# A gate table built from bfloat16 one-hots and a gate in three bfloat16 parts, one product moved from GpSimd to VectorE, and routing of one token block put first

## The chip, the core and the metric

The kernel runs on one NeuronCore of a Trainium2 chip. The metric is the device time of one execution in microseconds. TensorE is called PE below, VectorE DVE, ScalarE ACT, GpSimd POOL and SyncE SP, as in the profile. DVE, ACT, POOL and SP each take their instructions in the order in which the program put them.

## What is computed

One decoder block over 528 tokens (16 meta tokens and 512 of the sequence) of width 2048: a mixer (differential attention beside an mLSTM), then a PEER layer, both added to the residual stream, and a final RMS norm. The change lies in the PEER layer, which works on the 512 tokens that are kept:

```python
q = (ht @ w_q).reshape(T, PEER_HEADS, 2, PEER_SUB_DIM)            # 8 heads
s = jnp.einsum('thpd,hpnd->thpn', q, sub_keys)
s1, i1 = lax.top_k(s[:, :, 0], 16); s2, i2 = lax.top_k(s[:, :, 1], 16)
cand_s = s1[..., :, None] + s2[..., None, :]
cand_i = i1[..., :, None] * 128 + i2[..., None, :]
best_s, best_pos = lax.top_k(cand_s.reshape(T, 8, 256), 16)
idx = ...   # 128 experts of 16384 for a token
gate = jax.nn.softmax(best_s, axis=-1)
...
act = jax.nn.gelu(jnp.einsum('td,tkd->tk', hb, u[ib]), approximate=False)
y   = jnp.einsum('tk,tkd->td', gb * act, v[ib])
```

## The kernel before

Tokens lie in four blocks of 128. The kernel treats blocks 0 to 2 (384 tokens, `ND`) densely: it multiplies them with all 16384 rows of `u` and of `v`, and a table `G` holds each token's gate at the experts that it chose and zero elsewhere. Block 3 (128 tokens) is treated sparsely: for each of its 128 choices the rows of `u` are gathered by an indirect DMA on POOL's queue (`dgather`, 1 MB into one of three `ug` buffers), and DVE multiplies them with the token and sums up (`dmul`, a **dot**). Later the same is done with the rows of `v`.

The large matmuls are done in three passes of split float32 (`mm3`: high times high, high times low, low times high). So each weight tile of 1 MB comes in two halves, each loaded by SP into one of three `raw` buffers, rounded to a high part on ACT (`hid`, line 76) and subtracted on DVE to a low part (`lod`, line 77); five buffers hold high halves, and five low ones.

The stages that matter here:

- **Queries and routing.** `step(n)` for n = 2 to 15 multiplies a tile of `wq`; `scores` makes the scores of a head, and `bgstep` does one step of routing on DVE, ACT and POOL: the top 16 of two score rows, sums of candidates (`cd`, POOL), their top 16, and the expert numbers (`oh` on POOL, `ids` on DVE). There are 32 tasks, 8 heads by 4 blocks, in a pipeline of three. DVE's order in this stage is that of the code.
- **Chunks of `u`.** `u_chunk(c)` for c = 0 to 127 is 48 matmuls of 384 columns into one of two `pu` banks, a GELU on ACT (`at`, line 854) and a store into `Ad` in DRAM. The first chunks run beside what is left of routing, one `bgstep` each. Then come the exp and the sums of the gate, and transposes of expert numbers and gates (`n1T`, `n2T`, `ghT`, `glT`).
- **Gate table.** From then on each chunk is followed by about one gate group `gbuild(q)` of four tokens, 96 in all: `ebuild` compares an iota with the two halves of the expert number (`e`, `eq`, DVE), POOL multiplies `eq` with the high and the low part of the gate (`eg`), PE multiplies `e` with both (`pg`, four matmuls of 256 columns), ACT copies one half out and DVE adds the other (`stg`). After each eight groups SP stores `stg`, of which there is one buffer, into `Gd` (2 MB). The dots of block 3 are put between the chunks, about 1.2 a chunk. Here only PE and POOL keep the order of the code; a scheduler orders DVE, ACT and SP when the program is built.
- **Product with `v`.** `p_mul` multiplies `Ad` with `Gd` (`tm`, POOL), `p_split` splits the product (`ah` on ACT, `al` on DVE), and PE multiplies with all of `v` (`py`), while the gathered rows of `v` are added for block 3 on DVE (`y`).

Of the kernel before, what the change touches and what calls it, by code (L numbers as in the profile page):

```python
# [57 lines left out]
def body(tc, I, out):  # L58
    nc = tc.nc
    top = ExitStack()  # L60
    with top:
# [603 lines left out]
def rest(tc, I, out, L):  # L665
# [142 lines left out]
    n1T = up.tile([128, ND], F, name="n1T")
    n2T = up.tile([128, ND], F, name="n2T")
    ghT = up.tile([128, ND], R, name="ghT")  # L810
    glT = up.tile([128, ND], R, name="glT")
    bg = []
# [14 lines left out]

    nd = [0, 0]

    def dots(n):  # L830
        while nd[1] < min(n, 128):
            if nd[0] < 128 and nd[0] - nd[1] < 3:
                dgather(nd[0])
                nd[0] += 1
            else:
                dmul(nd[1])
                nd[1] += 1

    def step(n, mid=None):
        if n + 1 < len(sp):  # L840
# [16 lines left out]
    with tc.tile_pool(name="tk", bufs=1) as tk, \  # L857
# [33 lines left out]

        def head_tasks(h, b):
# [63 lines left out]
        pipe = [None, None]  # L956

        def bgstep():
            cur = bg.pop(0) if bg else None
            a, b = pipe  # L960
            if b:
                b[4]()
            topk16((cur[0]() if cur else []) + (a[2]() if a else []))
            if cur:
                cur[1]()
            if a:
                a[3]()
            pipe[:] = [cur, pipe[0]]
# [6 lines left out]
            for _ in range(1 + n % 2):  # L975
                bgstep()
        ci = 0
        while bg or pend or any(pipe):
            u_chunk(ci, mid)
            ci += 1  # L980
            bgstep()
        for g in (gsel, gs[:, 0], gs[:, 1], gs[:, 2]):
            g3 = g.rearrange("p (h k) -> p h k", h=PH)
            mx = tk.tile([128, PH], F, name="gmx", tag="gmx", bufs=2)
# [18 lines left out]
        for src, dst in ((n1s, n1T), (n2s, n2T), (gs, None)):  # L1003
            pt = ptr.tile([128, ND], F, name="ptt", tag="ptt")
            for b in range(3):
                nc.tensor.transpose(pt[:, 128 * b:128 * b + 128], src[:, b, :], ident)
            if dst is not None:
                nc.scalar.copy(dst, pt)
            else:
                nc.scalar.copy(ghT, pt)  # L1010
                nc.vector.tensor_tensor(glT, pt, ghT.bitcast(F), op=OP.subtract)

    with tc.tile_pool(name="gk", bufs=1, reuse_waits="tile") as gk, \
            tc.tile_pool(name="psg", bufs=2, space=PSUM) as psg, \
# [4 lines left out]

        def ebuild(q):  # L1020
            t0 = 4 * q
            e1 = gk.tile([128, 4, 128], R, name="e1", tag="e1", bufs=2)
            eq = gk.tile([128, 4, 128], F, name="eq", tag="eq", bufs=2)
            eg = gk.tile([128, 4, 2, 128], R, name="eg", tag="eg", bufs=2)
            io = bcast_mid(iota, 4)
            nc.vector.tensor_tensor(e1, io, bcast(n1T[:, t0:t0 + 4], 128), op=OP.is_equal)
            nc.vector.tensor_tensor(eq, io, bcast(n2T[:, t0:t0 + 4], 128), op=OP.is_equal)
            nc.gpsimd.tensor_tensor(eg[:, :, 0, :], eq, bcast(ghT[:, t0:t0 + 4].bitcast(F), 128), op=OP.mult)
            nc.gpsimd.tensor_tensor(eg[:, :, 1, :], eq, bcast(glT[:, t0:t0 + 4].bitcast(F), 128), op=OP.mult)
            ge[q] = e1, eg  # L1030

        def gbuild(q):
# [1 line left out]
            if r == 0:  # L1034
                stg[tg] = gk.tile([128, NK, TG], F, name="stg", tag="stg")
            e1, eg = ge.pop(q)
            pg = psg.tile([128, 4, 2, 128], F, name="pg", tag="pg")
            for j in range(4):
                nc.tensor.matmul(pg[:, j].rearrange("p a b -> p (a b)"), e1[:, j, :],  # L1039
                                 eg[:, j].rearrange("p a b -> p (a b)"), start=True, stop=True)  # L1040
            so = stg[tg][:, :, r:r + 4]
            nc.scalar.copy(so, pg[:, :, 0, :].rearrange("p j n -> p n j"))
            nc.vector.tensor_tensor(so, so, pg[:, :, 1, :].rearrange("p j n -> p n j"), op=OP.add)
            if r + 4 == TG:
                nc.sync.dma_start(Gd[tg, :, 0:NK, :], stg[tg])

# [15 lines left out]
    with ExitStack() as sV:  # L1062
# [279 lines left out]
```

## Time and profile before

| | |
|---|---|
| time, median of 3 runs (lowest to highest) | 3402.59 us (3402.31 to 3407.22) |
| the profiled execution: its own time, which is its span | 3404.6 us |
| PE busy | 3356.0 us, 99% |
| DVE busy | 2396.9 us, 70% |
| ACT busy | 1208.3 us, 35% |
| POOL busy | 1249.8 us, 37% |
| moved by DMA | 755.13 MB, mean 222 GB/s |

The busy share of an engine is a mean over stages with different limits, and the ends of matmuls are modelled in the trace, so the pace of PE is better read from the GELU that follows each chunk. The granted clock of PE is given as a share of its full 2.4 GHz; 0.5 is the lower of its two levels.

### The profile page before, as it was taken

How to read it: one execution, taken by the hardware profiler on the slowest of the kernel's cores; microseconds unless marked ns; L12 is line 12 of the kernel's file. 1: busy time of each engine (PE TensorE's matmuls, PEld its weight loads, DVE VectorE, ACT ScalarE, POOL GpSimd, SP SyncE). 2: the span in 40 equal slices, each digit the busy share in tenths (PEclk: the TensorE clock that was granted, in tenths of full speed). 3: DMA queues.
4: the chain of work that ended last, by engine and by line, in shares of the span. 5: the costliest groups of instructions: out<-in, count | busy, mean ns of one | idle time of the engine just before them, and what ended most of it. 6: DMA issues, size and time to landing. Idle time of an engine off the chain costs nothing.

```text
span 3404.6 us, 46653 instructions
## 1 busy us (share of the span) xinstructions
PE 3356.0 (99%) x17906; PEld 2983.9 (88%) x17910; DVE 2396.9 (70%) x3278; ACT 1208.3 (35%) x1851; POOL 1249.8 (37%) x1197
## 2 busy tenths in 40 slices
PE   8999999999998998999999999999999999999998
PEld 8888898888887798999999999998888888888887
DVE  7444444353467878888888888845788878888885
ACT  6443444352342224333333333332323333333333
POOL 2020111110025566655555555412444333334432
PEclk9999999999999999999999999999999999999999
DMA  4222221223442247888888888887878888888973
GB/s 151 75 69 75 67 76 63 69 69 118 169 147 80 80 133 252 305 313 320 299 332 304 311 300 319 317 274 256 312 290 315 307 316 306 306 310 307 330 291 140
DMA packets 225310, 755.13 MB, mean 222 GB/s; under 512 B 20640, under 2 KB 88736, under 8 KB 190272
## 3 DMA queue, kind: packets, MB, share of 16 engines
q1 hardware_dynamic: 106064, 402.82, 33.6%
q0 software_dynamic: 36864, 268.45, 20.3%
q10 hardware_dynamic: 82160, 80.90, 7.1%
q8 instruction: 140, 2.29, 0.3%
q14 instruction: 82, 0.67, 0.1%
HBM read 693.36 MB, written 58.72 MB: 221 GB/s over the span
## 4 chain that ended last, share of the span: by engine, by line
PE 88%; DVE 7%; POOL 3%; issue 1%; ACT 1%; DMA 1%; SPq 0%; DVEq 0%; ACTq 0%; POOLq 0%
PE py L1195 11%; PE py L1197 10%; PE py L1196 10%; PE pu L87 10%; PE pu L86 10%; PE pu L88 10%; PE ps L86 5%; PE ps L88 5%; PE ps L87 5%; PE po L742 2%; PE po L740 2%; PE po L741 2%; DVE ids L939 1%; PE pg L1039 1%; DVE lod L77 1%
## 5 line engine op out<-in xcount | busy, mean ns | idle before, releaser
L86 PE MATMUL pu<-hh,hid 128*128 128x384 f32 (+1 forms) x2272 | 786.0, 346 | 5.5 <-ACT at L854 5.5
L87 PE MATMUL pu<-hh,lod 128*128 128x384 f32 (+1 forms) x2272 | 788.2, 347 | 0.0
L88 PE MATMUL pu<-hl,hid 128*128 128x384 f32 (+1 forms) x2272 | 781.2, 344 | 0.0
L1195 PE MATMUL py<-hiv,ah 128*128 128x512 f32 x1536 | 613.0, 399 | 0.6 <-ACT at L854 0.6
L1197 PE MATMUL py<-hiv,al 128*128 128x512 f32 x1536 | 605.2, 394 | 0.0
L1196 PE MATMUL py<-lov,ah 128*128 128x512 f32 x1536 | 602.1, 392 | 0.0
L76 ACT CAST hiv<-rawv 128x1024 fp32r<-128x1024 f32 x256 | 268.6, 1049 | 522.1 <-PE py L1197 492.5
L76 ACT CAST hid<-rawd 128x1024 fp32r<-128x1024 f32 x284 | 297.0, 1048 | 426.2 <-DMA rawd<-in_u_dram 327.4
L77 DVE TENSOR_TENSOR lod<-rawd,hid 128x1024 fp32r<-128x1024 f32 x284 | 396.2, 1403 | 69.0 <-ACT hid L76 68.6
L86 PEld LDWEIGHTS pu<-hh,hid 128*128 128x128 f32 x2272 | 430.4, 189 | 15.7 <-ACT at L854 5.8
L88 PEld LDWEIGHTS pu<-hl,hid 128*128 128x128 f32 x2272 | 432.1, 190 | 10.2
L87 PEld LDWEIGHTS pu<-hh,lod 128*128 128x128 f32 x2272 | 430.6, 190 | 9.6
L86 PE MATMUL ps<-xh,hiz 128*128 128x256 f32 (+2 forms) x1280 | 410.6, 321 | 0.6 <-DVE qT L368 0.5
L1136 POOL DMA_INDIRECT vg<-in_vn_dram,ids x128 | 219.9, 1718 | 493.0 <-DVE y L1144 480.2
L88 PE MATMUL ps<-xl,hiz 128*128 128x256 f32 (+2 forms) x1280 | 392.6, 307 | 0.0
L87 PE MATMUL ps<-xh,loz 128*128 128x256 f32 (+2 forms) x1280 | 392.1, 306 | 0.0
L823 DVE SCALAR_TENSOR_TENSOR ug<-ug,h2n 128x2048 f32<-128x2048 f32 x128 | 314.1, 2454 | 92.2 <-DMA ug<-in_un_dram,idx 91.7
L1197 PEld LDWEIGHTS py<-hiv,al 128*128 128x128 f32 x1536 | 288.3, 188 | 75.2
L1196 PEld LDWEIGHTS py<-lov,ah 128*128 128x128 f32 x1536 | 288.3, 188 | 68.6
L1195 PEld LDWEIGHTS py<-hiv,ah 128*128 128x128 f32 x1536 | 288.3, 188 | 67.2 <-ACT at L854 0.9
L77 DVE TENSOR_TENSOR lov<-rawv,hiv 128x1024 fp32r<-128x1024 f32 x256 | 323.3, 1281 | 28.5 <-ACT hiv L76 28.3
L1144 DVE SCALAR_TENSOR_TENSOR y<-vg,wsel,y 128x2048 f32<-128x2048 f32 x127 | 336.1, 2646 | 0.0
(313 smaller groups left out, 4797.9 us busy)
## 6 DMA issues: line engine op xcount, KB each, us to landing
rawd<-in_u_dram SPq DMA_DIRECT2D x256, 512.0 KB
rawv<-in_v_dram SPq DMA_DIRECT2D x256, 512.0 KB
rawz<-in_wz_dram SPq DMA_DIRECT2D x98, 512.0 KB
Ad<-at ACTq DMA_DIRECT2D x128, 192.0 KB
Gd<-stg SPq DMA_DIRECT2D x12, 2048.0 KB
gt<-Gd ACTq DMA_DIRECT2D x32, 768.0 KB
av<-Ad ACTq DMA_DIRECT2D x64, 384.0 KB
rawwo<-in_wo_dram SPq DMA_DIRECT2D x40, 512.0 KB
```

Source lines behind the costliest of these rows:

```text
L76: nc.scalar.copy(hi, raw)
L77: eng.tensor_tensor(lo, raw, hi.bitcast(F), op=OP.subtract)
L86: nc.tensor.matmul(ps, a, xh[k][:, cs], start=(k == 0), stop=False)
L87: nc.tensor.matmul(ps, b, xh[k][:, cs], start=False, stop=False)
L88: nc.tensor.matmul(ps, a, xl[k][:, cs], start=False, stop=(k == KD - 1))
L740: nc.tensor.matmul(ps[tb], mh[n][:, sl], h, start=(n == 0), stop=False)
L823: nc.vector.scalar_tensor_tensor(ug, ug, 1.0, h2n, op0=OP.mult, op1=OP.mult, accum_out=act[:, k:k + 1])
L1136: nc.gpsimd.indirect_dma_start(out=vg, out_offset=None, in_=I["vn"], in_offset=bass.IndirectOffsetOnAxis(ap=ids2[:, k:k + 1], axis=0))
L1144: nc.vector.scalar_tensor_tensor(y[:, 3, :], vg, wsel[:, k:k + 1], y[:, 3, :], op0=OP.mult, op1=OP.add)
L1195: nc.tensor.matmul(ps[tb], ah[:, sl], h, start=(pr + j == 0), stop=False)
L1196: nc.tensor.matmul(ps[tb], ah[:, sl], l, start=False, stop=False)
L1197: nc.tensor.matmul(ps[tb], al[:, sl], h, start=False, stop=(2 * pr + j == GC - 1))
```

## The change

Four things are changed. The gate is split into three bfloat16 parts, kept as three float32 rows `gp`; the one-hots `e1` and `eq` are bfloat16 and lie with the four tokens innermost; ACT scales `eq` by each part of the gate (12 activations of 128 columns for a group), PE adds the three products up in PSUM (12 matmuls of 128 columns), and ACT alone copies the result. `p_mul` goes from POOL to DVE. The routing tasks of block 3 of all heads go into a list `first`, which is emptied before the other blocks are. And when block 3 is routed, two dots take the place of the routing step after each second chunk.

```diff
+    iota4 = up.tile([128, 128, 4], BF, name="iota4")
+    nc.vector.tensor_copy(iota4, bcast(iota, 4))
+    gp = up.tile([128, 3, ND], F, name="gp")
+    bg, first, routed = [], [], []
...
+    def dfetch():
+        while nd[0] < 128 and nd[0] - nd[1] < 3:
+            dgather(nd[0])
+            nd[0] += 1
+
     def dots(n):
         while nd[1] < min(n, 128):
-            if nd[0] < 128 and nd[0] - nd[1] < 3:
-                dgather(nd[0])
-                nd[0] += 1
-            else:
-                dmul(nd[1])
-                nd[1] += 1
+            dfetch()
+            dmul(nd[1])
+            nd[1] += 1
...
-                for b in (3, 0, 1, 2):
+                first.append(head_tasks(h, 3))
+                for b in range(3):
                     bg.append(head_tasks(h, b))
...
-            cur = bg.pop(0) if bg else None
+            q = first or bg
+            cur = q.pop(0) if q else None
...
-        while bg or pend or any(pipe):
+        while bg or first or pend or any(pipe):
             u_chunk(ci, mid)
+            if len(routed) < PH:
+                bgstep()
+                if len(routed) == PH:
+                    dfetch()
+            elif ci % 2:
+                dots(nd[1] + 2)
+            else:
+                bgstep()
             ci += 1
-            bgstep()
...
-                nc.scalar.copy(ghT, pt)
-                nc.vector.tensor_tensor(glT, pt, ghT.bitcast(F), op=OP.subtract)
+                rest_ = pt
+                for i in range(3):
+                    gb = tk.tile([128, ND], BF, name="gb", tag="scr", bufs=9)
+                    nc.scalar.copy(gb, rest_)
+                    nc.scalar.copy(gp[:, i, :], gb)
+                    if i < 2:
+                        r = tk.tile([128, ND], F, name="gr", tag="scr", bufs=9)
+                        nc.vector.tensor_tensor(r, rest_, gp[:, i, :], op=OP.subtract)
+                        rest_ = r
...
-            nc.vector.tensor_tensor(e1, io, bcast(n1T[:, t0:t0 + 4], 128), op=OP.is_equal)
-            nc.vector.tensor_tensor(eq, io, bcast(n2T[:, t0:t0 + 4], 128), op=OP.is_equal)
-            nc.gpsimd.tensor_tensor(eg[:, :, 0, :], eq, bcast(ghT[:, t0:t0 + 4].bitcast(F), 128), op=OP.mult)
-            nc.gpsimd.tensor_tensor(eg[:, :, 1, :], eq, bcast(glT[:, t0:t0 + 4].bitcast(F), 128), op=OP.mult)
+            e1 = gk.tile([128, 128, 4], BF, name="e1", tag="e1", bufs=2)
+            eq = gk.tile([128, 128, 4], BF, name="eq", tag="eq", bufs=2)
+            eg = gk.tile([128, 4, 3, 128], BF, name="eg", tag="eg", bufs=2)
+            nc.vector.tensor_tensor(e1, iota4, bcast_mid(n1T[:, t0:t0 + 4], 128), op=OP.is_equal)
+            nc.vector.tensor_tensor(eq, iota4, bcast_mid(n2T[:, t0:t0 + 4], 128), op=OP.is_equal)
+            for j in range(4):
+                for i in range(3):
+                    nc.scalar.activation(eg[:, j, i, :], eq[:, :, j], AF.Copy, scale=gp[:, i, t0 + j:t0 + j + 1])
...
             for j in range(4):
-                nc.tensor.matmul(pg[:, j].rearrange("p a b -> p (a b)"), e1[:, j, :],
-                                 eg[:, j].rearrange("p a b -> p (a b)"), start=True, stop=True)
-            so = stg[tg][:, :, r:r + 4]
-            nc.scalar.copy(so, pg[:, :, 0, :].rearrange("p j n -> p n j"))
-            nc.vector.tensor_tensor(so, so, pg[:, :, 1, :].rearrange("p j n -> p n j"), op=OP.add)
+                for i in range(3):
+                    nc.tensor.matmul(pg[:, j, :], e1[:, :, j], eg[:, j, i, :], start=(i == 0), stop=(i == 2))
+            nc.scalar.copy(stg[tg][:, :, r:r + 4], pg.rearrange("p j n -> p n j"))
...
-            nc.gpsimd.tensor_tensor(tm.rearrange("p (a t) -> p a t", t=TG),
+            nc.vector.tensor_tensor(tm.rearrange("p (a t) -> p a t", t=TG),
```

The change also moves instructions that it does not name. Three places show it.

The first is POOL's queue in the gate stage. Before, some way into the stage, products (`eg`) and gathers (`ug`) take turns:

```order
L1028 TENSOR_TENSOR eg<-eq,ghT 128x4x128
L1029 TENSOR_TENSOR eg<-eq,glT 128x4x128
L818 DMA ug<-in_un_dram,idx 128x2048 x2
L1028 TENSOR_TENSOR eg<-eq,ghT 128x4x128
L1029 TENSOR_TENSOR eg<-eq,glT 128x4x128
L818 DMA ug<-in_un_dram,idx 128x2048
L1028 TENSOR_TENSOR eg<-eq,ghT 128x4x128
L1029 TENSOR_TENSOR eg<-eq,glT 128x4x128
```

After, this is the queue from the last steps of routing to the gathered rows of `v`:

```order
L906 TENSOR_TENSOR cd<-sif 128x6
L908 TENSOR_TENSOR cd<-sif 128x8
L938 TENSOR_TENSOR oh<-eqb,cd 128x800
L819 DMA ug<-in_un_dram,idx 128x2048 x2
L938 TENSOR_TENSOR oh<-eqb,cd 128x800
L819 DMA ug<-in_un_dram,idx 128x2048 x107
L1154 DMA vg<-in_vn_dram,ids_75 128x2048 x128
L1188 TENSOR_TENSOR y<-y,nlw 128x512 x6
```

All gathers but those of the routing stage now follow one another, with no other work between them, and the products of `p_mul` no longer stand among the gathers of `v`.

The second is DVE's queue in the gate stage. Before, these are the rows for two chunks (`ug,act` is a dot, `e_` and `eq` are the one-hots, `stg` is the add, and the numbers of `lod_0` and `lod_1` tell the tiles apart):

```order
L823 SCALAR_TENSOR_TENSOR ug,act<-ug,h2n 128x2048
L1043 TENSOR_TENSOR stg<-stg,pg 128x128x4
L77 TENSOR_TENSOR lod_0_14943<-rawd_0_14940,hid_0_14942 128x1024
L1027 TENSOR_TENSOR eq<-iota,n2T 128x512
L77 TENSOR_TENSOR lod_1_14949<-rawd_1_14946,hid_1_14948 128x1024
L823 SCALAR_TENSOR_TENSOR ug,act<-ug,h2n 128x2048
L1026 TENSOR_TENSOR e_15014<-iota,n1T 128x512
L77 TENSOR_TENSOR lod_0_15024<-rawd_0_15021,hid_0_15023 128x1024
L1043 TENSOR_TENSOR stg<-stg,pg 128x128x4
L1027 TENSOR_TENSOR eq<-iota,n2T 128x512
L77 TENSOR_TENSOR lod_1_15030<-rawd_1_15027,hid_1_15029 128x1024
```

After, these are the rows for two chunks, in the first third of the stage:

```order
L1046 TENSOR_TENSOR eq<-iota_9064,n2T 128x512
L824 SCALAR_TENSOR_TENSOR ug,act<-ug,h2n 128x2048
L1045 TENSOR_TENSOR e_14694<-iota_9064,n1T 128x512
L77 TENSOR_TENSOR lod_0_14714<-rawd_0_14711,hid_0_14713 128x1024
L824 SCALAR_TENSOR_TENSOR ug,act<-ug,h2n 128x2048 x2
L77 TENSOR_TENSOR lod_1_14720<-rawd_1_14717,hid_1_14719 128x1024
L1046 TENSOR_TENSOR eq<-iota_9064,n2T 128x512
L824 SCALAR_TENSOR_TENSOR ug,act<-ug,h2n 128x2048
L1045 TENSOR_TENSOR e_14793<-iota_9064,n1T 128x512
L77 TENSOR_TENSOR lod_0_14813<-rawd_0_14810,hid_0_14812 128x1024
L824 SCALAR_TENSOR_TENSOR ug,act<-ug,h2n 128x2048
```

The add is gone, and three dots stand between one pair of `lod` and the next, where one or two stood. After the `lod` of chunk 58 DVE's queue holds no dot any more; before, they reach to chunk 117.

The third is ACT's queue between two GELUs (`at`) of the gate stage, before:

```order
L854 ACTIVATE at<-pu 128x384
L76 CAST hid_0_14696<-rawd_0_14694 128x1024
L855 DMA Ad<-at 128x384
L1042 COPY stg<-pg 128x128x4
L76 CAST hid_1_14702<-rawd_1_14700 128x1024
L854 ACTIVATE at<-pu 128x384
```

and after:

```order
L857 ACTIVATE at<-pu 128x384
L76 CAST hid_0_15601<-rawd_0_15599 128x1024
L858 DMA Ad<-at 128x384
L1061 COPY stg<-pg 128x128x4
L1049 ACTIVATE eg<-eq,gp 128x128 x12
L76 CAST hid_1_15607<-rawd_1_15605 128x1024
L857 ACTIVATE at<-pu 128x384
```

The 12 activations that make `eg` for the next group stand behind the copy of this group's `pg` and ahead of the second half of `hid`.

## Rows read from the trace of the kernel before

**Rows 1.** Part 1 of the page: busy time, share and instructions of each engine.
```profile
PE 3356.0 (99%) x17906; PEld 2983.9 (88%) x17910; DVE 2396.9 (70%) x3278; ACT 1208.3 (35%) x1851; POOL 1249.8 (37%) x1197
```

**Rows 2.** Windows: length, busy time (instructions), PE's clock, DMA share, GB/s.
```profile
core 0: us, PE busy (x) PEld busy (x) DVE busy (x) ACT busy (x) POOL busy (x), PEclk, DMA share, GB/s
980.00:1180.00 200.00, 182.16 (x818) 149.18 (x817) 154.70 (x616) 50.71 (x102) 113.50 (x329) 0.95 0.25 80
1227.00:1277.00 50.00, 50.00 (x286) 50.00 (x285) 39.30 (x149) 14.15 (x27) 31.80 (x77) 1.00 0.38 126
1290.00:1300.00 10.00, 7.92 (x30) 7.92 (x31) 5.92 (x18) 9.50 (x13) 0.00 (x0) 0.66 0.39 119
1320.00:1330.00 10.00, 5.70 (x24) 5.37 (x23) 10.00 (x10) 2.01 (x3) 9.26 (x5) 0.76 0.81 297
1340.00:2220.00 880.00, 880.00 (x5126) 879.79 (x5125) 760.27 (x722) 289.83 (x388) 497.38 (x306) 1.00 0.85 312
2320.00:3380.00 1060.00, 1059.75 (x4542) 852.62 (x4543) 846.47 (x702) 329.12 (x398) 412.60 (x258) 1.00 0.80 298
```

**Rows 3.** Timeline of ACT: GELU starts of chunks 0, 16, 110, 111, 123, 124.
```profile
1185.16 0.49 ACT L854 ACTIVATE at<-pu 128x384 f32<-128x384 f32 x1 [3.24 <-PE pu L88]
...
1337.95 0.49 ACT L854 ACTIVATE at<-pu 128x384 f32<-128x384 f32 x1 [3.17 <-PE pu L88]
...
2173.70 0.49 ACT L854 ACTIVATE at<-pu 128x384 f32<-128x384 f32 x1 [0.98 <-PE pu L88]
...
2182.61 0.49 ACT L854 ACTIVATE at<-pu 128x384 f32<-128x384 f32 x1 [1.64 <-PE pu L88]
...
2285.89 0.49 ACT L854 ACTIVATE at<-pu 128x384 f32<-128x384 f32 x1 [3.18 <-PE pu L88]
...
2294.34 0.49 ACT L854 ACTIVATE at<-pu 128x384 f32<-128x384 f32 x1 [3.18 <-PE pu L88]
```

**Rows 4.** Chain that ended last, in order of time: start, length.
```profile
128.34 1.09 PE po L457 x8
```

**Rows 5.** Groups by line on DVE and ACT, 1227 to 1277 and 1340 to 2220 us.
```profile
L77 DVE TENSOR_TENSOR lod<-rawd,hid 128x1024 fp32r<-128x1024 f32 x11 | 13.0, 1217 | 0.0
L939 DVE TENSOR_REDUCE ids<-oh 128x16 f32<-128x800 f32 x5 | 7.7, 1541 | 10.4 <-POOL oh L934 10.4
...
L823 DVE SCALAR_TENSOR_TENSOR ug<-ug,h2n 128x2048 f32<-128x2048 f32 x124 | 302.5, 2440 | 88.2 <-DMA ug<-in_un_dram,idx 87.7
L1043 DVE TENSOR_TENSOR stg<-stg,pg 128x512 f32<-128x512 f32 x94 | 63.8, 678 | 10.2 <-ACT stg L1042 10.2
...
L1042 ACT COPY stg<-pg 128x512 f32<-128x512 f32 x93 | 54.3, 584 | 65.1 <-DMA Gd<-stg 50.3 <-DVE lod L77 14.8
...
L987 ACT ACTIVATE gs<-gs x3: 310/310/313, 1293.3 to 1299.3; 128x128 f32<-128x128 f32 x3
```

**Rows 6.** Groups by line on POOL, 1340 to 2220 us; all gathers of `ug`.
```profile
L1028 POOL TENSOR_TENSOR eg<-eq,ghT 128x512 fp32r<-128x512 f32 x92 | 132.1, 1436 | 341.7 <-PE pg L1039 339.6 <-DVE eq L1027 2.1
...
DMA to landing us min/median/max: 5.9/7.4/15.1
```

**Rows 7.** DMA, 1340 to 2220 us.
```profile
DMA packets 61854, 274.67 MB, mean 312 GB/s; under 512 B 6868, under 2 KB 19540, under 8 KB 44767
q1 hardware_dynamic: 29967, 126.41, 39.8%
q0 software_dynamic: 17568, 127.93, 39.1%
```

**Rows 8.** DMA, 1340 to 1540 us, in 40 slices; issues, us to landing.
```profile
GB/s 323 209 419 313 224 334 262 242 329 213 272 386 400 423 267 204 260 332 219 397 409 239 271 417 336 390 322 417 397 305 214 283 238 299 232 346 229 376 358 172
...
ug<-in_un_dram,idx POOLq DMA_INDIRECT x29, 9.4
```

**Rows 9.** Groups by line on POOL and DVE, 2320 to 3380 us.
```profile
L1082 POOL TENSOR_TENSOR tm<-av,gt 128x384 f32<-128x384 f32 x118 | 175.4, 1487 | 171.5 <-DVE al L1094 99.3 <-issue 70.2
...
L1094 DVE TENSOR_TENSOR al<-tm,ah 128x384 fp32r<-128x384 f32 x120 | 84.9, 708 | 0.0
```

More of the change, by code (lines that the diff above doesn't have):

```diff
@@ L807, in rest @@
     nc.scalar.dma_start(iota, I["c_iota"])
[L808 to L812, printed above, removed]
+    iota4 = up.tile([128, 128, 4], BF, name="iota4")
+    nc.vector.tensor_copy(iota4, bcast(iota, 4))
+    n1T = up.tile([128, ND], BF, name="n1T")
+    n2T = up.tile([128, ND], BF, name="n2T")
+    gp = up.tile([128, 3, ND], F, name="gp")
+    bg, first, routed = [], [], []
     ugs = {}
@@ L941, in t3 @@
                     nc.vector.tensor_copy(idx[:, cs], ids[:, 3, cs])
+                    routed.append(h)
             return t1, t1b, t2, t2b, t3
@@ L1021, in ebuild @@
             t0 = 4 * q
[L1022 to L1025, printed above, removed]
-            nc.vector.tensor_tensor(e1, io, bcast(n1T[:, t0:t0 + 4], 128), op=OP.is_equal)
-            nc.vector.tensor_tensor(eq, io, bcast(n2T[:, t0:t0 + 4], 128), op=OP.is_equal)
-            nc.gpsimd.tensor_tensor(eg[:, :, 0, :], eq, bcast(ghT[:, t0:t0 + 4].bitcast(F), 128), op=OP.mult)
-            nc.gpsimd.tensor_tensor(eg[:, :, 1, :], eq, bcast(glT[:, t0:t0 + 4].bitcast(F), 128), op=OP.mult)
+            e1 = gk.tile([128, 128, 4], BF, name="e1", tag="e1", bufs=2)
[6 more added lines that the diff above has]
+                    nc.scalar.activation(eg[:, j, i, :], eq[:, :, j], AF.Copy, scale=gp[:, i, t0 + j:t0 + j + 1])
             ge[q] = e1, eg
@@ L1036, in gbuild @@
             e1, eg = ge.pop(q)
-            pg = psg.tile([128, 4, 2, 128], F, name="pg", tag="pg")
+            pg = psg.tile([128, 4, 128], F, name="pg", tag="pg")
             for j in range(4):
-                nc.tensor.matmul(pg[:, j].rearrange("p a b -> p (a b)"), e1[:, j, :],
-                                 eg[:, j].rearrange("p a b -> p (a b)"), start=True, stop=True)
-            so = stg[tg][:, :, r:r + 4]
-            nc.scalar.copy(so, pg[:, :, 0, :].rearrange("p j n -> p n j"))
-            nc.vector.tensor_tensor(so, so, pg[:, :, 1, :].rearrange("p j n -> p n j"), op=OP.add)
+                for i in range(3):
+                    nc.tensor.matmul(pg[:, j, :], e1[:, :, j], eg[:, j, i, :], start=(i == 0), stop=(i == 2))
+            nc.scalar.copy(stg[tg][:, :, r:r + 4], pg.rearrange("p j n -> p n j"))
             if r + 4 == TG:
```

## The prediction

> **What bounds the kernel now.** I read the busy line of the page first: TensorE is busy for 3356.0 of 3404.6 us, and no other engine passes 70% [rows 1]. A busy share hides how fast an engine runs, so I then cut the span by stage: from 1340 to 2220 us, the gate stage, PE is busy for all 880 us at full clock while the 16 DMA engines are busy 0.85 of the time; in the stage on `v` PE is busy for 1059.75 of 1060 us [rows 2]. The places where PE stands lie between 980 and 1330 us, while routing runs (the windows of [rows 2] up to 1330 us). The period of a chunk comes from the starts of its GELU: 8.45 us without a gate group and 8.91 us with one [rows 3]. So one gate group, 4 matmuls of 256 columns, costs 0.46 us of PE. PE sets the end, and an edit counts only where it changes PE's own work or makes PE wait.
>
> Span and time agree: 3404.6 us is the profiled execution's own time, 2.0 us above the median of the three runs (3402.59); nothing lies around it that I have to add. The sum is made against 3404.6.
>
> **PE's work per gate group.** Before, 1024 columns; after, 12 matmuls of 128, so 1536 columns. At the present rate per column that is 0.46 x 1.5 = 0.69 us, the lower bound. The only row for a run of short matmuls is 8 of 128 columns (float32) in 1.09 us, 0.136 us each [rows 4], so 1.63 us is the upper bound. The nearest is the lower one, the rate of the kernel's own matmuls of 256 to 512 columns; but each short matmul comes with its own weight load of 128 columns, so I take 0.80. That is +0.34 us x 96 = **+33 us** (bounds +22 and +112). The Trainium skill (TensorE: Matmul & The Clock Gate, Back-to-back issue gap) has about 81 ns for one of a stream of weight load and matmul pairs of 128 columns; by that a group is 0.97 us and the term +49 us. No row here shows such a bfloat16 stream.
>
> **Routing.** PE loses time between GELU 0 and GELU 16: 1337.95 - 1185.16 = 152.8 us [rows 3] for 16 chunks of 8.45 and two gate groups, 136 us; the difference is 17 us, of which I leave 2 to the 9 transposes. The loss is 15 us: PE waited for GELU behind the exp of the gate, whose input DVE finished late, then for the first `eg` on POOL, each followed by slow clock (0.66 and 0.76 in [rows 2]). After, a routing step stands only in every second chunk, with two dots in the other, and `eg` leaves POOL. DVE is busy 39.3 us for five routing chunks [rows 2], 7.9 each; the rest of their 50 us it waits for `oh` (10.4 us, [rows 5]), which by the next chunk but one is long there. A dot chunk takes 2 x 2.44 + 2 x 1.22 = 7.3 us. Both lie under 8.45. I give back the whole 15: **-15 us** (bounds 0 and -15). The 14 steps on `wq` before it keep 21 routing steps in both versions; their loss (PE busy 182 of 200 us) stays.
>
> **The dots after that.** This is the term that decides. Before, POOL's queue holds two `eg` products between the gathers, and these wait for `pg` on PE: 339.6 us of waiting [rows 6]. The gathers, and so the dots on DVE, are paced by PE at 1.2 a chunk. After, POOL has no product there: 107 gathers stand in one run, each waiting only for the dot three before it. DVE's order (fixed when the program is built) then packs the dots as close as it can: 18 stand ahead of the `lod` of chunk 22, 26 between chunks 22 and 27, 84 between 28 and 58, 2.7 a chunk, none later. DVE takes its queue in order, so a `lod` behind a dot waits for that dot's gather, and PE waits for `lod`.
>
> What the gathers need: 110 x 1.049 MB (128 x 2048 x 4 B) = 115 MB. The 37 chunks in that stretch load 1.049 MB of `u` and write 0.197 MB to `Ad`, 46 MB, and four gate stores of 2.1 MB make 8: 169.6 MB. From 1340 to 2220 us the queues moved 274.67 MB [rows 7] in 0.85 x 880 = 748 us of busy engines, 367 GB/s. At that rate with no gap: **462 us**. PE needs for the same chunks 37 x 8.45 + 33 x 0.80 + 4 = 343 us, and DVE enters with lods for an estimated chunk and a half ready, 13 us. PE stands for 462 - 343 - 13 = **+106 us**. Bounds: the highest 5 us slices show 417 to 423 GB/s [rows 8], so 401 us and +45; the mean that this kernel really reached, 312, gives 544 us and +188. A check without bytes: three `ug` buffers, a gather that lands 9.4 us after issue in a busy stretch [rows 8], 2.4 us of dot; (9.4 + 2.4 + about 0.3)/3 = 4.0 us a dot, 444 us in all. I take 462. The Trainium skill (DMA: Bandwidth & Descriptors, Measured (HBM→SBUF, 128 partitions, SWDGE, issued from GpSimd)) gives 425 GB/s for a 16 MB transfer while the neighbour core idles and 341 for 1 MB; 425 would make the stretch 399 us and the stand +43. The slices of [rows 8] agree with it for 5 us at a time, and no row holds it for 50.
>
> **Other edits.** On ACT 12 small activations per group stand between the copy of `pg` and the next `hid`. A 128x128 activation lasts 0.31 us [rows 5], of which about 0.1 overlaps the next, so 2.4 to 3.7 us more beside 2.9 us of 8.91 (290 us in 880, [rows 2]): ACT stays below 75%. Their cover is the whole chunk between `eg` and its matmuls. It is gone four times, where two groups follow one chunk: `pg` then waits for GELU, `hid`, copy and 12 activations, about 4 us. Two of the four lie outside the stretch, and the GELU of `act`, now in the middle of ACT's queue, waits for the last dot: **+8 us** (0 to 20). The wait for the single `stg` buffer (50.3 us in all, [rows 5]) now also holds `eg`; but the copy is the last writer now, so the store no longer waits for DVE's add, and outside the stretch no gathers compete with it: 0 (to 20, in the 8's upper end). On DVE the add into `stg` goes (0.68 us) and the one-hots shrink; DVE was not the bound there, so 0. In the `v` stage the product moves from POOL (1.49 us) to DVE, where a TENSOR_TENSOR of that shape takes 0.71 us [rows 9]: 120 x 0.71 = 85 us on an engine busy 846 of 1060. Its cover is PE at 1059.75 of 1060; 0, and if the cover were gone, what passes 1060, at most some tens of us.
>
> **Sum:** 3404.6 + 33 - 15 + 106 + 8 = **3537 us**.
>
> **Rivals.** (a) The gathers keep up and no `lod` is late: 3404.6 + 33 - 15 + 8 = 3431. For it speaks that DVE waited for gathers only 88 us of 880 [rows 5]; against it, that 110 dots in 343 us would need 169.6/343 = 494 GB/s, above the highest slice. (b) Faster: as (a), with short matmuls that cost no more than the old ones, a group at 0.55 us or less, and no wait on ACT: 3404.6 - 15 + 9 = 3398. The point from which it decides is 0.55 us; below 0.69 the columns would have to run faster than any now, and (a) must hold too. (c) Waiting PE falls to the lower clock: at half speed a chunk of 48 matmuls takes 16.9 us, so 37 take 625 us and the groups twice 26; if the whole stretch ran so, the stand were 678 - 343 - 13 = 322 us and the end 3753; the routing stage, with PE idle a tenth of the time, had 0.95 [rows 2], so at most a part of it. (d) The loop of three buffers binds rather than bytes: at 15.1 us, the slowest gather in [rows 6], 110 x (15.1 + 2.7)/3 = 653 us, about 3728; at the 11 us that lies between, 502 us and 3577.
>
> **How the numbers follow.** The forecast, a stand set by gathers, gets 0.85: 0.80 for 3465 (rate of the fastest slices, short matmuls at 0.69) to 3615 (the mean rate), 0.05 above it by (c) or (d). Rival (a) has 0.10, (b) 0.03, and 0.02 is left for anything near no change. A measurement here can tell about 0.2%, 7 us. Slower than that 0.95, within it 0.02, faster 0.03. The range is 3465 to 3615.
>
> **What would show it.** In the profile after: GELU periods near 8.45 up to chunk 20, then about 12 us and uneven up to chunk 58, then 9.2 to 9.3; DVE idle before `ug` dots grown from 88 to some hundreds of us, and PE waiting for DVE's `lod`, with granted clock below 1 in that stretch alone; DMA busy 0.95 or more there and under 0.5 after the last dot; no `ug` after chunk 60; PE per group 0.7 to 1.0 us; the `v` stage the same length within 3 us. I am wrong if the stretch runs at PE's pace (a), if the groups cost more than 1.1 us, or if the `v` stage grows by DVE's new product.

## The result, and the profile after

The changed kernel takes 3526.06 us (median of 4 runs, 3521.66 to 3530.0), the kernel before beside it 3404.15 us (3402.31 to 3407.22): a ratio of 1.0358, 95% interval 1.0343 to 1.0372, 122 us slower. The profiled execution after has a span of 3528.2 us.

Lines of the page after: the busy line of PE, then granted clock, DMA share and GB/s in 40 slices of 88 us.

```profile
PE 3403.9 (96%) x18674; PEld 3007.4 (85%) x18678; DVE 2192.0 (62%) x3312; ACT 1553.9 (44%) x3008; POOL 840.3 (24%) x877
...
PEclk9999999999999998899999999999999999999999
DMA  4222222223532478999974545466788888888974
GB/s 155 70 72 68 70 72 67 66 90 120 199 119 78 162 285 319 343 378 377 375 285 161 166 162 183 159 225 215 286 306 306 312 307 319 303 303 317 328 291 143
```

PE is busy 48 us longer, and 76 us more of the span lies outside its busy time. In slices 17 to 20 the DMA engines are full (343 to 378 GB/s), and in slices 22 to 26 about half idle: the gathers of `ug` have been packed into that stretch. The windows after (columns as in [rows 2]; the last two are the longest stand of PE, and the stretch from GELU 22 to GELU 59, on which the prediction makes its sum):

```profile
1350.00:1400.00 50.00, 23.64 (x135) 23.31 (x133) 43.06 (x50) 14.70 (x17) 22.67 (x12) 0.78 0.88 338
1400.00:1450.00 50.00, 32.74 (x164) 29.31 (x165) 40.10 (x54) 29.09 (x77) 17.42 (x15) 0.71 0.86 309
1450.00:1800.00 350.00, 307.19 (x1865) 293.09 (x1864) 276.29 (x286) 200.31 (x488) 99.15 (x81) 0.93 0.98 378
1850.00:2300.00 450.00, 450.00 (x2959) 441.83 (x2959) 162.78 (x199) 323.73 (x810) 0.00 (x0) 1.00 0.51 167
2320.00:3380.00 1060.00, 1058.97 (x4732) 874.80 (x4731) 782.29 (x778) 330.88 (x401) 279.12 (x120) 1.00 0.83 298
1373.00:1412.00 39.00, 0.79 (x5) 0.46 (x4) 31.83 (x49) 7.26 (x10) 15.76 (x11) 0.56 0.95 351
1370.10:1825.40 455.30, 368.87 (x2210) 350.51 (x2209) 356.77 (x390) 260.75 (x633) 128.90 (x102) 0.89 0.95 360
```

PE, which never stood from 1340 to 2220 us before, loses in two places that look different. From 1350 to 1450 us it works little more than half the time; most of that loss lies from 1373 to 1412 us, where it stands and the DMA engines are at 0.95. From 1450 to 1800 us it loses 43 of 350 us, and they are full (0.98, 378 GB/s over 350 us). From 1850 us on it stands no more, and the `v` stage is as before. The granted clock is below 1 in all of the packed stretch: 0.78, 0.71 and 0.93 in the first three windows. From 1450 to 1800 us 1865 matmuls take 307 us; at the pace of e1 below (2292 in 350 us at clock 1.00) they would take 285, by an estimate from the two windows. So part of the 48 us is the same work at a lower clock, and the gate groups are 25 of them (below).

The GELU starts after, ACT's timeline, for chunks 0, 16, 23, 24, 59, 60, 114, 115, 116 and 117 (they answer to [rows 3]):

```profile
1182.44 0.50 ACT L857 ACTIVATE at<-pu 128x384 f32<-128x384 f32 x1
...
1314.51 0.49 ACT L857 ACTIVATE at<-pu 128x384 f32<-128x384 f32 x1 [1.37 <-PE pu L88]
...
1383.44 0.49 ACT L857 ACTIVATE at<-pu 128x384 f32<-128x384 f32 x1
1429.86 0.49 ACT L857 ACTIVATE at<-pu 128x384 f32<-128x384 f32 x1
...
1825.39 0.56 ACT L857 ACTIVATE at<-pu 128x384 f32<-128x384 f32 x1
1834.33 0.49 ACT L857 ACTIVATE at<-pu 128x384 f32<-128x384 f32 x1 [2.41 <-PE pu L88]
...
2331.25 0.49 ACT L857 ACTIVATE at<-pu 128x384 f32<-128x384 f32 x1 [2.70 <-PE pu L88]
2340.43 0.49 ACT L857 ACTIVATE at<-pu 128x384 f32<-128x384 f32 x1 [3.17 <-PE pu L88]
2349.60 0.49 ACT L857 ACTIVATE at<-pu 128x384 f32<-128x384 f32 x1 [3.17 <-PE pu L88]
2358.05 0.49 ACT L857 ACTIVATE at<-pu 128x384 f32<-128x384 f32 x1 [3.18 <-PE pu L88]
```

A chunk with a gate group takes 9.17 us, one without 8.45: a group costs 0.72 us, 0.26 more than before. Chunks 0 to 16 take 132.1 us instead of 152.8. And one single step, chunk 23 to 24, takes 46.4 us. The waits of the whole span after (total, times, longest):

```profile
POOL ug L819 <- DVE ug L824: 278.4, 89, 8.3
ACT hid L76 <- DMA rawd<-in_u_dram: 131.0, 46, 7.4
DVE ug L824 <- DMA ug<-in_un_dram,idx: 91.5, 56, 7.4
...
PE ptt L1019 <- DVE n1s L1010: 38.2, 1, 38.2
...
PE pu L87 <- DVE lod L77: 18.2, 11, 2.3
...
PE pg L1060 <- DVE e L1045: 16.5, 3, 10.7
...
PE pg L1060 <- ACT eg L1049: 6.7, 3, 2.4
```

PE waits once for 38.2 us: its order is that of the code, and there stand the transposes (`ptt`) of the expert numbers `n1s`. DVE's timeline shows what `n1s` stands behind (start, length, idle before):

```profile
1382.72 2.29 DVE L824 SCALAR_TENSOR_TENSOR ug<-ug,h2n 128x2048 f32<-128x2048 f32 x1 [0.74 <-DMA ug<-in_un_dram,idx]
1384.94 0.08 DVE L824 DVE_READ_ACCUMULATOR ug<-ug,h2n 128x1 f32 x1
1384.94 0.28 DVE L1001 TENSOR_REDUCE gmx<-gs 128x8 f32<-128x128 f32 x1
1385.14 1.22 DVE L77 TENSOR_TENSOR lod<-rawd,hid 128x1024 fp32r<-128x1024 f32 x1
1386.27 0.20 DVE L1002 RECIPROCAL gmx<-gmx 128x8 f32<-128x8 f32 x1
1386.38 2.24 DVE L824 SCALAR_TENSOR_TENSOR ug<-ug,h2n 128x2048 f32<-128x2048 f32 x1
1388.55 0.09 DVE L824 DVE_READ_ACCUMULATOR ug<-ug,h2n 128x1 f32 x1
1388.55 0.29 DVE L1003 TENSOR_TENSOR gs<-gs,gmx 128x128 f32<-128x128 f32 x1
...
1411.44 0.36 DVE L1010 CAST n1s<-ju 128x384 f32<-128x384 uint32 x1
```

The gating is a chain of short operations (0.2 to 0.4 us), and the scheduler has put dots between its links, each of 2.3 us and some with a wait for a gather on top: 12 between the first link and `n1s`, ten of them while PE stands.

### The profile page after: what moved, and what is told of

It reads as the page before. It is cut to its first block, busy times and chain, and to the rows that moved or that the text cites. A ratio compares the mean times of both kernels' runs of the same rounds, so it can differ in the third digit from the quotient of the medians.

```text
span 3528.2 us, 48789 instructions
## 1 busy us (share of the span) xinstructions
PE 3403.9 (96%) x18674; PEld 3007.4 (85%) x18678; DVE 2192.0 (62%) x3312; ACT 1553.9 (44%) x3008; POOL 840.3 (24%) x877
## 4 chain that ended last, share of the span: by engine, by line
PE 80%; issue 8%; POOL 4%; DVE 3%; DMA 3%; ACT 1%; POOLq 0%; SPq 0%; ACTq 0%; DVEq 0%
PE py L1214 10%; PE py L1213 10%; PE py L1215 10%; PE pu L86 8%; PE pu L87 8%; PE pu L88 8%; PE ps L86 5%; PE ps L88 5%; PE ps L87 5%; POOL ug L819 3%; PE po L742 2%; PE po L740 2%; PE po L741 2%; DMA ug<-in_un_dram,idx 1%; PE pg L1060 1%
## 5 line engine op out<-in xcount | busy, mean ns | idle before, releaser
L87 PE MATMUL pu<-hh,lod 128*128 128x384 f32 (+1 forms) x2272 | 792.5, 349 | 18.4 <-DVE lod L77 18.2
L86 PE MATMUL pu<-hh,hid 128*128 128x384 f32 (+1 forms) x2272 | 796.8, 351 | 2.6 <-ACT at L857 2.6
L1154 POOL DMA_INDIRECT vg<-in_vn_dram,ids x128 | 299.9, 2343 | 1344.8 <-DVE y L1162 655.1
L1214 PE MATMUL py<-lov,ah 128*128 128x512 f32 x1536 | 612.8, 399 | 0.5 <-DVE lov L77 0.5
L1213 PE MATMUL py<-hiv,ah 128*128 128x512 f32 x1536 | 605.4, 394 | 0.6 <-ACT at L857 0.6
L86 PEld LDWEIGHTS pu<-hh,hid 128*128 128x128 f32 x2272 | 433.8, 191 | 13.7 <-ACT at L857 3.7
L77 DVE TENSOR_TENSOR lod<-rawd,hid 128x1024 fp32r<-128x1024 f32 x284 | 350.0, 1242 | 119.6 <-ACT hid L76 119.3
L1049 ACT ACTIVATE eg<-eq,gp 128x128 bf16<-128x128 bf16 x1152 | 357.6, 411 | 2.1 <-DVE eq L1046 2.1
L824 DVE SCALAR_TENSOR_TENSOR ug<-ug,h2n 128x2048 f32<-128x2048 f32 x128 | 292.0, 2288 | 91.9 <-DMA ug<-in_un_dram,idx 91.5
```

The source lines that it names most:

```text
L77: eng.tensor_tensor(lo, raw, hi.bitcast(F), op=OP.subtract)
L86: nc.tensor.matmul(ps, a, xh[k][:, cs], start=(k == 0), stop=False)
L87: nc.tensor.matmul(ps, b, xh[k][:, cs], start=False, stop=False)
L824: nc.vector.scalar_tensor_tensor(ug, ug, 1.0, h2n, op0=OP.mult, op1=OP.mult, accum_out=act[:, k:k + 1])
L1049: nc.scalar.activation(eg[:, j, i, :], eq[:, :, j], AF.Copy, scale=gp[:, i, t0 + j:t0 + j + 1])
L1154: nc.gpsimd.indirect_dma_start(out=vg, out_offset=None, in_=I["vn"], in_offset=bass.IndirectOffsetOnAxis(ap=ids2[:, k:k + 1], axis=0))
```

## The experiments

The table gives the time, its ratio to the kernel before, run beside it on the same chip (95% interval), and the us between the GELU starts of the chunks named, which show where the time lies. Of 0 to 127 in the kernel before, 1073.7 us would be bare chunks (127 x 8.454).

| kernel | us | ratio | 0-16 | 20-25 | 25-59 | 59-64 | 64-116 |
|---|---|---|---|---|---|---|---|
| before | 3404.2 | | 152.8 | 49.9 | 297.6 | 44.0 | 464.8 |
| after | 3526.1 | 1.0343-1.0372 | 132.1 | 97.2 | 379.9 | 45.6 | 478.6 |
| e1 DVE in code order | 3421.9 | 1.0027-1.0055 | 131.2 | 52.7 | 313.7 | 46.4 | 478.1 |
| e2 routing alone | 3395.7 | 0.9954-0.9979 | 131.5 | 52.4 | 304.2 | 44.6 | 464.7 |
| e3 gate alone | 3670.5 | 1.0750-1.0787 | 284.0 | 57.9 | 322.9 | 45.9 | 474.1 |
| e4 half gathers | 3482.2 | 1.0202-1.0234 | 131.1 | 100.3 | 327.0 | 45.9 | 478.6 |
| e5 gating clear | 3509.3 | 1.0283-1.0315 | 132.2 | 53.2 | 389.9 | 59.6 | 476.7 |
| e6 clear, half gathers | 3450.4 | 1.0113-1.0144 | 132.0 | 53.5 | 338.0 | 53.2 | 476.8 |
| e7 e1, 8 matmuls a group | 3402.8 | 0.9977-0.9995 | 132.4 | 53.6 | 307.0 | 45.4 | 466.0 |
| e8 e2, DVE in code order | 3478.3 | 1.0200-1.0230 | 132.3 | 50.9 | 337.4 | 46.6 | 515.0 |
| e9 e2, product on DVE | 3395.3 | 0.9962-0.9984 | 131.3 | 52.3 | 303.5 | 45.5 | 463.5 |
| e10 e2, gating clear | 3408.8 | 0.9999-1.0017 | 131.4 | 54.2 | 312.4 | 45.6 | 463.4 |
| e11 e6, two slabs | 3450.9 | 1.0114-1.0145 | 131.1 | 52.7 | 339.3 | 52.8 | 477.6 |
| e12 clear, quarter gathers | 3423.8 | 1.0034-1.0067 | 131.8 | 53.1 | 321.0 | 51.3 | 475.1 |

**e1.** The dots are spread again, the rest of the change stays.

```diff
-            tc.manual_schedule(engines={mybir.EngineType.Pool}):
+            tc.manual_schedule(engines={mybir.EngineType.Pool, mybir.EngineType.DVE}):
```

> The changed kernel with VectorE, like GpSimd, issuing the gate stage in the order of the code: the U dots then stand one a chunk from chunk 24 to chunk 111, where the changed kernel has two to four a chunk up to chunk 58. Theory A (the packed gathers need more bytes than the DMA engines move, and the weights of U come late): the loss of about 117 us between GELU 0 and GELU 127 falls back to about the 17 us of before, less the routing stalls; what stays is the dearer gate group, 96 x 0.26 = 25 us; 3404.6 - 15 + 25 = 3415 us (3405 to 3430). Theory B (the loss is the three-buffer loop of gathers and dots, or ScalarE's twelve activations a group, whatever the gathers' rate): the loop and the activations are still there, so 3500 us or more.

3421.9 us: theory A's forecast. The window of e1 from 1450 to 1800 us, as the one of after above:

```profile
1450.00:1800.00 350.00, 350.00 (x2292) 343.68 (x2292) 210.87 (x239) 252.00 (x621) 52.32 (x43) 1.00 0.82 294
```

PE stands no more, with the same 12 activations on ACT and the same three buffers. So 104.2 us of the change's cost (3526.1 - 3421.9) come from DVE's order in the gate stage and what follows from it. The edit fixes that whole order, the dots and also the one-hots and the low halves; what the order costs, e4 to e6 and e12 take apart.

**e2.** Only the routing and the dots put first, as in the first four hunks of the change; gate and `v` stage as before.

> The kernel before with only the routing of block 3 and the U dots put first; gate table and v stage as before. In VectorE's order 18 dots then stand among the routing and one a chunk follows to chunk 110. Prediction's own term: the stalls of the routing go, -15 us, 3390 us (3383 to 3398), since GpSimd's gate products still pace the gathers. Rival: the dots that come earlier meet the heads' operations on VectorE and cost what they save: 3400 to 3410 us, no change.

-10.4 us. Chunks 0 to 16 give back 21 us, and chunks 20 to 59 take 9 of them again; PE's own waits there are 5.6 us (see e10).

**e3.** Gate edits alone, on the routing loop of before.

> The changed kernel with the routing loop and the v stage's product as before: only the gate table is changed. In VectorE's order all 128 dots then stand in some 42 chunks, 3 a chunk. Theory A: 42 chunks of U at 1.55 MB and 128 gathers of 1.05 MB are 199 MB, 543 us at the 367 GB/s of the prediction, against some 380 us of matmuls: about +150, +25 for the gate groups, 3580 us (3530 to 3610). Rival (the packing, and with it the loss, comes from putting the U dots first, not from the gate table): 3404.6 + 25 = 3430 us (3415 to 3445).

The rival is out: the packing comes from the gate edit, which takes the `eg` products out of POOL's queue. But the size, and the place, were not as theory A had them: GELU 0 comes at 1271.3 us instead of 1185.2, and 44 of the 128 dots run before it, among the steps on `wq`. Waits of e3 from 1180 to 1500 us:

```profile
ACT hid L76 <- DMA rawd<-in_u_dram: 139.4, 23, 10.7
PEld pu L87 <- DVE lod L77: 131.9, 17, 22.0
PE pu L87 <- DVE lod L77: 126.1, 17, 21.6
ACT sif L921 <- DVE si L880: 96.2, 18, 14.6
DVE ids L942 <- POOL oh L937: 62.4, 19, 3.8
```

With routing unfinished the packed dots stand among its steps on DVE, and chunks 1 to 11 take 14.4 to 17.0 us each. DMA is busy only 0.65 of that stretch (238 GB/s), and PE waits 126 us for `lod`. That speaks for the turn on DVE rather than for bytes; no run takes the two apart here.

**e4.** The changed kernel with gathers of half the bytes. (The diff leaves out the factor 2 on `idx` and its inverse.)

```diff
-        nc.gpsimd.indirect_dma_start(out=ug, out_offset=None, in_=I["un"],
+        nc.gpsimd.indirect_dma_start(out=ug[:, D // 2:], out_offset=None, in_=I["un"].rearrange("r (a c) -> (r a) c", a=2),
...
-        nc.vector.scalar_tensor_tensor(ug, ug, 1.0, h2n, op0=OP.mult, op1=OP.mult, accum_out=act[:, k:k + 1])
+        u2 = bass.AP(tensor=ug.tensor, offset=ug.offset + D // 2, ap=[list(ug.ap[0]), [0, 2], [1, D // 2]])
+        nc.vector.scalar_tensor_tensor(ug.rearrange("p (a c) -> p a c", a=2), u2, 1.0, ...
```

> The changed kernel with gathers of half a row of un (1024 of 2048 columns; the dot reads that half twice, so it lasts as long and its sum is another): order, buffers, waits and the number of transfers stay, their bytes are halved. Theory A (bytes): chunks 22 to 58 move 169.6 - 56 = 113 MB, 309 us at 367 GB/s, less than the 343 us of matmuls, so most of the 67 us lost in chunks 25 to 59 comes back, and a part of the 52 us of chunks 20 to 25: 3526 - 67 - 20 = 3440 us (3420 to 3470). Theory B (the loop of three buffers, its latency and VectorE's order): the latency of a gather falls little, 3500 to 3526 us.

Neither: 3482.2. In chunks 25 to 59 it does what theory A says (379.9 to 327.0). In chunks 20 to 25 nothing comes back (97.2 and 100.3). But the order did not stay, though the expectation says so: the scheduler ordered DVE anew, and 16 dots instead of 12 now stand between the first link of the gating and `n1s`. DVE waits less for gathers from 1340 to 1450 us (15.4 us instead of 22.5), and PE waits longer:

```profile
PE ptt L1020 <- DVE n1s L1011: 42.6, 1, 42.6
```

So there are two losses, and halved bytes don't mend the first. What bytes alone would do to it under the same order e4 can't say; e5 takes the dots away instead.

**e5.** No dot between the links of the gating; packed as in the changed kernel after that. `man` is a region whose DVE instructions keep the order of the code. The gating stands in it, but the dots are written behind it, and the scheduler was free to move them up; the edit takes the first two chunks with dots into such a region too.

```diff
-        man.close()
         u_chunk(ci)
...
+        man.close()
...
+        man = ExitStack()
+        man.enter_context(tc.manual_schedule(engines={mybir.EngineType.DVE}))
         ebuild(0)
         for c in range(ci, NK - UTAIL):
+            if c == ci + 2:
+                man.close()
             u_chunk(c)
```

> The changed kernel with VectorE held to the order of the code from the routing to the second chunk of the gate stage, and free after it: no U dot then stands among the exponentials' subtractions, sums and products and the splitting of the numbers (the chain n1s ends), where the changed kernel has a dot between almost every two; the other dots stay packed, 2 to 4 a chunk, now up to chunk 64. Theory AB (two losses: the transposes wait for n1s behind some 14 dots, and after that the gathers' bytes): the wait of 38 us at the transposes goes, but the dots that it hid come later, 20 more in the stretch that is bound by bytes: 3526 - 52 + 20 = 3494 us (3475 to 3510), and GELU 23 to 24 no longer takes 46 us. Theory A (bytes alone): the same bytes through the same DMA, 3515 to 3530. Theory B (order alone): 3526 - 50 = 3476 or less, with the steps from chunk 25 on as after.

The step of 46 us is gone (97.2 to 53.2), as theory AB has it; but only 16.8 us are left of these 44, since chunks 25 to 64 now take 24 us more: gathers that went on during the wait now fall into later chunks. Windows of e5:

```profile
1400.00:1450.00 50.00, 50.00 (x332) 49.00 (x332) 41.28 (x43) 33.02 (x83) 14.24 (x12) 1.00 0.97 371
1450.00:1500.00 50.00, 47.19 (x279) 44.74 (x279) 38.47 (x41) 27.57 (x66) 13.30 (x11) 0.93 1.00 394
```

**e6.** Both edits, e4 and e5.

> The edit that clears the gating and the gathers of half a row together (the dot reads its half twice, so its sum is another). Theory AB: both losses are gone; what is left is the dearer gate groups, 3404.6 - 15 + 25 + some 10 = 3425 us (3418 to 3440), about what VectorE in the order of the code gave (3421.9). Rival (three buffers, gather latency and the dots' turn on VectorE still bind in the packed stretch, whatever the bytes): 3450 or more.

3450.4, 28 us above e1: the rival's side of the line, by its number. Two reasons were left for the 28 us, and e11 and e12 take them apart.

**e11.** e6 with `bufs=2` for `stg`.

> The kernel with the gating cleared and gathers of half a row (3450.4), and two buffers for the staged slab of G instead of one. Of its 28 us above the kernel in the order of the code, theory D lays most to the five writes of G: the copies into the slab wait on ScalarE for its write, and weights' high halves and the GELU stand behind them (18 us from GELU 39 to 40, 47 to 48, 61 to 62). With two slabs that wait is gone: 3450 - 20 = 3430 us (3420 to 3438). Rival E (the turns of dots, one-hots and low halves on VectorE and the gathers' latency): 3445 to 3452.

No difference, and DVE's order in the gate stage is the same as in e6, so theory D falls: the wait for the slab's store shows in the trace, but it is not what sets the pace.

**e12.** e5 with gathers of a quarter of a row.

> The kernel with the gating cleared, and gathers of a quarter of a row (the dot reads the quarter four times, so its sum is another). Halving the gathers took 59 us; 28 us are left above the kernel in the order of the code. Theory F (bytes still: in bursts the gathers, the weights and the writes of G together ask for more than the DMA gives): a half of these go, 3425 to 3438 us, and ScalarE's waits for weights, 78.6 us between 1410 and 1840 us with half rows, fall with it. Theory E (turns: packed dots, one-hots and low halves on VectorE and what stands behind them on ScalarE, whatever the bytes): 3446 to 3454 us, and these waits stay.

3423.8, as e1 within its scatter: theory F, and more of it than forecast. ACT's wait for weights from 1410 to 1840 us in e5, in e6 and in e12:

```profile
ACT hid L76 <- DMA rawd<-in_u_dram: 137.3, 42, 7.5
```
```profile
ACT hid L76 <- DMA rawd<-in_u_dram: 78.6, 34, 5.7
```
```profile
ACT hid L76 <- DMA rawd<-in_u_dram: 30.4, 17, 3.2
```

DVE's order in the gate stage, dots (2.28 us each) and one-hots are the same in all three; only the bytes of a gather fall, and with them DVE's wait for gathers (from 1450 to 1800 us 71.8, 35.6 and 18.4 us). The windows of e6 and of e12 in that stretch (e5 has 0.98 and 379 GB/s):

```profile
1450.00:1800.00 350.00, 326.66 (x2092) 318.27 (x2091) 304.74 (x323) 231.02 (x573) 128.24 (x87) 0.98 0.83 287
```
```profile
1450.00:1800.00 350.00, 342.19 (x2228) 335.57 (x2226) 311.24 (x331) 244.82 (x606) 134.26 (x87) 0.99 0.67 229
```

So of the 104.2 us, 16.8 go with the dots in the gating (after to e5), 85.5 with the size of the packed gathers (e5 to e12), and 1.9 are left, no more than the runs scatter. Of the 85.5, 58.9 go while the DMA engines come down from 0.98 to 0.83, and 26.6 more below that, where they are no longer full on average; whether these are bursts, as theory F has it, or the time that a gather takes to land is not shown. With half gathers, clearing the gating is worth 31.8 us (e4 to e6) instead of 16.8, but e4 has more dots there, so this is no clean measure of how far the two losses overlap.

**e7.** e1 with two parts of the gate in the sum (`range(2)` in the matmuls).

> The changed kernel with VectorE in the order of the code, and only two of the gate's three parts multiplied into the table (8 matmuls a group instead of 12; the third part is built and left out of the sum). If a group costs what its matmuls cost, 0.72 us / 12 = 0.06 us each, 96 x 4 x 0.06 = 23 us go: 3421.9 - 23 = 3399 us (3395 to 3403). Rival (a group costs a fixed switch of weights and a wait for its one-hots, whatever its matmuls): 3412 to 3422.

-19.1 us, so 384 matmuls cost 0.050 us each. A chunk steps by 8.87 to 8.98 us instead of 9.17, which makes 0.05 to 0.075 us for each of four matmuls. At 0.05, 12 of them are 0.60 of the group's 0.72 us; at 0.06 they are all of it. Most of a group's cost goes with the number of its matmuls; whether all of it does stays open.

**e8.** e2 with DVE in the order of the code, the edit of e1.

> The kernel before with the routing of block 3 and the U dots first, and VectorE in the order of the code in the gate stage; gate table and v stage as before. Routing alone gave 3395.7. The 11 us that GELU 20 to 21 loses there go, and the later stalls stay: 3385 to 3395 us. Rival (in the order of the code VectorE's addition of the low part waits for ScalarE's copy with the next weights' low halves behind it): 3400 or more.

The rival, and far beyond its number. Waits of e8 from 1410 to 1840 us:

```profile
POOL eg L1040 <- DVE eq L1039: 116.0, 45, 6.9
ACT hid L76 <- DMA rawd<-in_u_dram: 104.6, 53, 7.9
DVE stg L1055 <- ACT stg L1054: 62.8, 33, 5.7
PEld pg L1051 <- POOL eg L1041: 33.5, 14, 10.7
PE pg L1051 <- POOL eg L1041: 28.9, 11, 10.5
```

With the old gate DVE adds the low part to the slab, and in the order of the code it stands there for ACT's copy while one-hots and low halves wait behind it; the waits fit this, and no run takes the add alone away. The scheduler's order is the better one there, and the worse one after the change.

**e9.** e2 with `p_mul` on DVE.

> The kernel with the routing alone (3395.7), and the product of A and G in the v stage on VectorE instead of GpSimd: the third edit on top of the first. The prediction's term: TensorE is busy all of the v stage either way, so nothing: 3395.7 (3391 to 3400). Rival (VectorE's order in the v stage, with the product ahead of low halves, lets TensorE wait): 3405 or more.

No difference (3395.3 beside 3395.7), as forecast. e2 and e9 are the fastest versions found, 0.33% and 0.27% under the kernel before.

**e10.** e2 with the gating cleared, the edit of e5.

> The kernel with the routing alone, and VectorE held to the order of the code through the gating and two chunks of the gate stage; GpSimd's gate products pace the gathers after that as before. The step from GELU 20 to GELU 21 took 20.1 us there (the transposes wait for the numbers): it falls to about 10, and 3395.7 - 8 = 3388 us (3382 to 3394). Rival (the lost time is made up anyway, since weights lie ready later): 3395, no difference.

13 us slower than e2 instead of 8 faster. The step of 20 us from chunk 20 to 21 goes, but chunk 24 to 25 now takes 19.4 us and chunk 26 to 27 takes 16.9. The waits of e10 from 1385 to 1480 us show POOL late for the first gate groups:

```profile
POOL eg L1040 <- DVE eq L1039: 19.8, 3, 10.2
...
PE pg L1051 <- POOL eg L1041: 13.0, 2, 6.8
```

The two longest waits of PE in e2 from 1340 to 2220 us show why there was little to win:

```profile
PE pu L86 <- ACT at L856: 3.8, 1, 3.8
PE pg L1051 <- POOL eg L1041: 1.5, 1, 1.5
```

PE does not wait at the transposes there, though the expectation says so: the late GELU costs it 3.8 us. In e10 PE's waits in the same stretch are 13.7 us instead of 5.6 (with 0.7 and 0.3 for `stg`), and the profiled executions differ by the same 8 us (3404.7 and 3396.8); the rest of the 13 lies between these and the medians.

## Why the prediction was right, and where its reasons were not

The time (3526, forecast 3537) and the sign were right, and so was the main reason: packed dots and full DMA engines. That the sum came within 11 us is partly luck, since it held neither the wait in the gating nor the lower clock. The terms, one by one:

- **PE's work per gate group, +33.** Right in kind, a little large: 0.72 us against the 0.80 taken, near the lower bound of 0.69; 96 x 0.26 = +25. e1 beside e2 has +26.2 for it. The Trainium skill (TensorE: Matmul & The Clock Gate, Back-to-back issue gap) has 81 ns for a pair of weight load and matmul of 128 columns; here it is 60 ns with all the group's fixed cost (0.72/12), and 50 ns for each that e7 leaves out. The measurement decides.
- **Routing, -15.** The place gives 20.7 us (chunks 0 to 16), the edit alone 10.4 (e2): what I counted as saved is partly lost again in chunks 20 to 59. A wait for `eg` at the start of the gate stage, which the term gave back, is still there, at chunk 24 (below).
- **The dots after that, +106.** Measured 104.2 (after minus e1). The stretch between GELU 22 and GELU 59 lasted 455 us where I had 462, and over it 360 GB/s moved with the DMA engines at 0.95, where I had 367 with no gap; over 350 us of it they were at 0.98 with 378. The Trainium skill's 425 GB/s for a transfer of 16 MB (DMA: Bandwidth & Descriptors, Measured (HBM→SBUF, 128 partitions, SWDGE, issued from GpSimd)) was not reached over these 350 us. PE was busy 369 us of the 455 where I had 343, at a clock of 0.89. But the step that let bytes alone set that stretch was wrong in one part: DVE's order also put dots between the links of the gating, and PE's transposes stood 38.2 us for that, while the DMA engines were at 0.95 with 351 GB/s. I had listed the order and looked in it only for `lod`. From 1450 to 1800 us, too, PE waited 16.5 us for the one-hots `e` beside 18.2 for `lod`. The gating hardly moved the sum, because the gathers ran on during the wait: taken away, it gives 16.8 us, and the rest goes with the size of the gathers (e5, e12).
- **Other edits, +8.** Seen at one of the four places. Where two groups first follow one chunk, PE waits 2.4 us for `eg` and then takes the second group's matmuls as ACT finishes its activations, in 3.6 us instead of 0.86. The step from GELU 24 is 15.7 us, and 17.3 in e1, where this wait (3.5 us) is the only one of PE from 1380 to 2320 us. At the two places behind the stretch the step is 9.86 instead of 9.17 us: the second group's own 0.7 and no wait. 12 activations take 3.7 us and ACT is busy 200 of 350 us.
- **`v` stage, 0.** Confirmed by e9, and by PE's 1058.97 of 1060 us.
- **Rivals.** (a) fell for this order; with the dots spread it holds, and e1 has 3422 (forecast 3431). (b) fell with a group at 0.72 us. (c) shows in part, with a clock of 0.71 to 0.78 from 1350 to 1450 us and 0.93 from 1450 to 1800; what that adds to the time no run takes apart. (d), the loop of three buffers, can't be told from bytes by the gathers' size alone, since a smaller gather also ends DVE's wait sooner; the DMA engines at 0.98 speak for bytes. A run with more `ug` buffers, which would tell, was not made.
- **What would show it.** Uneven steps up to chunk 58, 9.17 behind them, DMA at 0.98 and then 0.51 (forecast under 0.5), no dot behind chunk 60: seen. Wrong was that DVE's idle time before dots would grow: over the whole span it is 91.5 us, before it was 91.7. The late transfers show one step earlier, in ACT's wait for the weights and POOL's for the dots.

## What to carry to other kernels

When work leaves an in-order queue, ask what it was pacing there. Here two products on GpSimd had spaced 1 MB gathers over some 90 chunks (e2), and without them a free scheduler packed 110 of them into 37. Read the new order of every in-order engine for all that the pinned engine waits for, not for the one tile that comes to mind; here a chain of short operations with long ones put between its links held PE for 38 us. Compare that order again before you read an experiment: an edit that only halves bytes made the scheduler order anew (e4). And a stall that overlaps a transfer-bound stretch is worth less than its length: price it by taking it away with the bound in place.

## What had not been expected of the hardware

The DMA engines held 378 GB/s over 350 us (after) with indirect gathers, loads, and 2 MB stores side by side, and 394 over 50 us (e5). One ScalarE activation that scales 128 strided bfloat16 columns takes 411 ns in the trace, and 12 in a row about 3.7 us, so some 0.1 us of each lies under the next.
